# Two half-height products side by side in the score stage of differential attention

## The chip, the core and the metric

The kernel runs on one NeuronCore of a Trainium2 chip. The metric is the device time of one execution in microseconds (us); lower is better. The median of three runs of the kernel before is 1331.72 us (1330.39 to 1333.47).

## The reference

One decoder layer of 1024 tokens and width 1024: one input projection, a group of four differential-attention heads and a group of eight sparse-attention heads, an output projection, a layer norm, a SwiGLU feed-forward layer and a second layer norm. The change touches the differential heads alone. Each has two parts `c` with queries and keys of 64 dimensions; their two softmax maps share the values and are subtracted:

```python
def block(args):                     # 128 query rows
    qi, q_blk = args
    ...
    s = jnp.einsum('bqhcd,bkhcd->bhcqk', q_blk, k).astype(f32) * scale
    s = s - slopes[None, :, None, None, None] * dist
    p = masked_softmax(s, dist >= 0)
    a = p[:, :, 0] - lam * p[:, :, 1]
    return jnp.einsum('bhqk,bkhe->bqhe', a.astype(dt), v)
```

## The kernel before

**Two-term numbers.** Large products work on float32r operands. A float32 tensor is split into a high term and the low rest, and a product of two such tensors is made of three products, high by high, high by low and low by high (`mm3`, lines L118 to L120).

**Scores.** A score product has only 64 dimensions, so the 128 rows of the array hold both terms of the key at once. For part 0 of a head, `kd[0]` has the key's high term in partitions 0 to 63 and its low term in 64 to 127; for part 1, `kd[1]` has them the other way round (`evac_k`). A query tile `q` holds its high term twice, once in each half of the partitions, in columns 0 to 511, and its low term twice in columns 512 to 1023 (`evac_q` writes one copy, and `move`, L163, makes the others with DMAs). `q_of` returns the two column ranges of a block of 128 query rows as `q[0]` (high) and `q[1]` (low).

`scores` then needs two products per chunk. The first (L313) is the high query by both terms of the key; the second (L314) is the low query by both terms of the key, and accumulates onto the first in one score bank of PSUM:

```python
nc.tensor.matmul(ps[:, :c + part], lhsT=q[0], rhs=k[:, ks], start=True, stop=False)
nc.tensor.matmul(ps[:, :c + part], lhsT=q[1], rhs=k[:, ks], start=False, stop=True)
```

**Chunks and banks.** A unit is one head and one block `i` of 128 query rows. Its width is `(i + 1) * 128` keys. A width up to 512 is one chunk, a greater one is two of equal size, so chunks have 128, 256, 384, 512, and twice 320, 384, 448 or 512 columns. Over four heads there are 48 chunks per part, 96 in all. There are two score banks (`ps_s`, tag S). For each chunk VectorE reads the bank, adds the distance term, writes the scores to a tile `t` and keeps the running minimum (L320); its last minimum is the bias of the exponential on ScalarE (`exps`, L334). A bank is free for the next chunk when L320 has read it.

**Order.** `front` of a unit (in `diff_units`) makes the scores and exponentials of part 0, then of part 1, then combines them (L451 to L457, VectorE and GpSimd). `back` transposes the combined map (L343), multiplies by the values (L470) and collects the head's output. The back of a unit is written one or two units after its front. Between them lie fillers: projections of later heads and of the output layer, whose products (L118 to L120 into the banks psM) have a lower priority, and which a pump deals out at a rate for each phase. The framework's scheduler sets each engine's final order from priorities and a model of the timeline. Each engine runs its instructions in that order, TensorE's weight loads (PEld in the profile) being able to run ahead of its products.

Of the kernel before, what the change touches and what calls it, by code (L numbers as in the profile page):

```python
# [11 lines left out]
F32 = mybir.dt.float32  # L12
F32R = mybir.dt.float32r
AF = mybir.ActivationFunctionType
ALU = mybir.AluOpType
AX = mybir.AxisListType

P = 128
# [21 lines left out]
def layer_kernel(ctx: ExitStack, tc: tile.TileContext, xT, x, w_t, w_vg, w_dv, lam_in, subln,  # L40
# [4 lines left out]
    nc = tc.nc  # L45
# [7 lines left out]
    def ps_s():  # L53
        return psum.tile([P, 512], F32, tag="S", name="psS", bufs=2)

    def ps_t():
        return psum.tile([P, 512], F32, tag="T", name="psT", bufs=3)

    def ps_o():
        return psum.tile([P, 512], F32, tag="O", name="psO", bufs=1)  # L60
# [85 lines left out]
    with ExitStack() as ctx_a:  # L146
        pa = ctx_a.enter_context(tc.tile_pool(name="pa", bufs=1))

        def small(shape, tag, bufs, dt=F32):
            return pa.tile(shape, dt, tag=tag, name=tag, bufs=bufs)  # L150
# [101 lines left out]
        dsel = pa.tile([P, 1024], F32, tag="dsel", name="dsel", bufs=1)  # L252
# [44 lines left out]
        def q_of(qt, i, a):  # L297

            q = qt[1 + i // 4][a]
            c = (i % 4) * P  # L300
            return q[:, c:c + P], q[:, 512 + c:512 + c + P]

        def scores(q, k, k0, width, dist, slope, m, t, cmp=None):

            c = NC if cmp else 0
            n = (c + width + 511) // 512
            w = -(-(c + width) // (32 * n)) * 32
            part, at = width - (n - 1) * w, 0
            m0 = None
            for h in range(n):  # L310
                ps = ps_s()
                ks = slice(k0 + at, k0 + at + part + c)
                nc.tensor.matmul(ps[:, :c + part], lhsT=q[0], rhs=k[:, ks], start=True, stop=False)  # L313
                nc.tensor.matmul(ps[:, :c + part], lhsT=q[1], rhs=k[:, ks], start=False, stop=True)  # L314
                if c:
                    k0 += c
                    nc.vector.tensor_tensor_reduce(out=cmp[0], in0=ps[:, :c], in1=cmp[1], scale=slope, scalar=3.0e38,
                                                   op0=ALU.add, op1=ALU.min, accum_out=cmp[2])
                m1 = m if h == n - 1 else pa.tile([P, 1], F32, tag="m0", name="m0", bufs=4)
                nc.vector.tensor_tensor_reduce(out=t[:, at:at + part], in0=ps[:, c:c + part],  # L320
                                               in1=dist[:, at:at + part], scale=slope,
                                               scalar=3.0e38 if h == 0 else m0, op0=ALU.add, op1=ALU.min,
                                               accum_out=m1)
                at, part, c, m0 = at + part, w, 0, m1

        def t_tiles(width):

            if width <= 512:
                t = pa.tile([P, 1024], F32, tag="t", name="t", bufs=6)
                return [t[:, 0:512], t[:, 512:1024]]  # L330
            return [pa.tile([P, 1024], F32, tag="t", name="t", bufs=6) for _ in range(2)]

        def exps(t, width, m, r):
            nc.scalar.activation(t[:, :width], t[:, :width], AF.Exp, bias=m, scale=-1.0, accum_out=r)  # L334
# [4 lines left out]
        def transposed_whole(srcs):  # L339

            tp = ps_t()
            for n, s in enumerate(srcs):
                nc.tensor.transpose(tp[:, n * P:(n + 1) * P], s, ident)  # L343
            w = len(srcs) * P
            pt = pt_tile(F32)
            nc.scalar.copy(pt[:, :w], tp[:, :w])
            return pt
# [84 lines left out]
        def diff_units(h, qt, kd, V):  # L432
            slope = SLOPES[h]
            state = {}

            def make(i):
                hf, i4 = divmod(i, 4)
                width = (i + 1) * P
                ts = []

                def front():
                    m = small([P, 2], "m", 4)
                    if i4 == 0:
                        state["r0", hf] = small([P, 4], "r0", 2)
                    r0, r1 = state["r0", hf][:, i4:i4 + 1], small([P, 1], "r1", 4)
                    ts.extend(t_tiles(width))
                    for c in range(2):
                        scores(q_of(qt, i, c), kd[c], 0, width, dsel[:, 1024 - width:], slope, m[:, c:c + 1], ts[c])
                        exps(ts[c], width, m[:, c:c + 1], r1 if c else r0)

                    nc.vector.reciprocal(r1, r1)  # L451
                    nc.vector.scalar_tensor_tensor(r1, r0, lam[:, 0:1], r1, op0=ALU.mult, op1=ALU.mult)
                    cut = width * 5 // 8
                    nc.vector.scalar_tensor_tensor(ts[0][:, :cut], ts[1][:, :cut], r1, ts[0][:, :cut],
                                                   op0=ALU.mult, op1=ALU.add)
                    nc.gpsimd.tensor_scalar(ts[1][:, cut:width], ts[1][:, cut:width], r1, None, op0=ALU.mult)
                    nc.gpsimd.tensor_add(ts[0][:, cut:width], ts[0][:, cut:width], ts[1][:, cut:width])  # L457

                def back(fill):
                    if i4 == 0:  # L460
                        state["orow"] = small([P, 4, P], "od", 2)
                        state["ss"] = small([P, 4], "ss", 2)
                    orow, ss = state["orow"], state["ss"]
                    po = ps_o()
                    for j4 in range(0, i + 1, 4):
                        js = range(j4, min(j4 + 4, i + 1))
                        pt = transposed_whole([ts[0][:, j * P:(j + 1) * P] for j in js])
                        for n, j in enumerate(js):
                            c = (j % 4) * 256 + (h % 2) * P
                            nc.tensor.matmul(po[:, :P], lhsT=pt[:, n * P:(n + 1) * P], rhs=V[j // 4][:, c:c + P],  # L470
                                             start=(j == 0), stop=(j == i))
                        fill((j4 + len(js)) / (i + 1))
                    tmp = small([P, P], "ms", 2)
                    nc.vector.tensor_copy(orow[:, i4, :], po[:, :P])
                    nc.scalar.activation(tmp, po[:, :P], AF.Square, accum_out=ss[:, i4:i4 + 1])
                    if i4 == 3:
                        late.append(lambda: finish(orow, ss, state["r0", hf]))

                def finish(orow, ss, r0):

                    nc.vector.tensor_mul(r0, r0, r0)
                    nc.vector.tensor_scalar(r0, r0, EPS, None, op0=ALU.mult)
                    nc.vector.scalar_tensor_tensor(ss, ss, 1.0 / P, r0, op0=ALU.mult, op1=ALU.add)
                    nc.gpsimd.tensor_tensor(ss, ss, mhalf[:, :4], op=ALU.pow)
                    nc.vector.tensor_mul(orow, orow, ss.unsqueeze(2).to_broadcast([P, 4, P]))
                    tp = ps_t()
                    for n in range(4):
                        nc.tensor.transpose(tp[:, n * P:(n + 1) * P], orow[:, n, :], ident)
                    for n in range(2):
                        md = small([P, 256], "tmp", 3)  # L490
                        nc.scalar.activation(md, tp[:, n * 256:(n + 1) * 256], AF.Copy, scale=g08)
                        b = hf * 4 + n * 2
                        nc.sync.dma_start(mix_d[b:b + 2, :, h, :].rearrange("i p t -> p i t"),
                                          md.rearrange("p (i t) -> p i t", t=P))

                return front, back, 2.0 * (i + 1) + 1

            return [make(i) for i in range(NB)]
# [186 lines left out]
        for hf in range(2):  # L685
            ps3 = [f() for f in (ps_s, ps_m, ps_t)]
            for k in range(KT):
                ks = slice(k * P, (k + 1) * P)
# [7 lines left out]
        kd = [[] for _ in range(4)]  # L696
# [4 lines left out]
        for k0, nk in ((0, 3), (3, 3), (6, 2)):  # L701
            n = nk * 280
# [10 lines left out]
        for i in range(NB):  # L713
# [3 lines left out]
            ps = ps_t()  # L717
# [82 lines left out]
        for make, fillers, due, after, look in phases:  # L800
# [26 lines left out]
            at = 0.0  # L827
# [390 lines left out]
```

## Time and profile before

| | |
|---|---|
| median of 3 runs | 1331.72 us |
| the profiled execution | 1330.62 us |
| its span, first to last instruction | 1328.9 us |
| granted TensorE clock, mean | 0.997 |
| TensorE busy | 1301.0 us (98%) |
| VectorE / ScalarE / GpSimd busy | 914.5 / 649.7 / 467.4 us |
| score products of all heads, L313 and L314 | 304 and 304 |

Busy time is the union of an engine's instructions. A line of a group reads: source line, engine, operation, output and inputs, shapes and count, then busy time in us, mean duration in ns, idle time just before, and what ended that idle time. A line of a timeline begins with the start and the duration in us. TensorE's products overlap in the pipeline, so a product's duration is longer than the distance to the next start.

### The profile page before, as it was taken

The page shows a single profiled execution, that of the slowest core. Times are in us where ns is not written, and L with a number is a line of the kernel's source. Part 1 is how long each engine was busy: PE and PEld are TensorE (multiplying, and loading weights), DVE is VectorE, ACT ScalarE, POOL GpSimd, SP SyncE. Part 2 cuts the span into 40 slices and gives each one's busy share as a digit, 9 for nine tenths or more (in the row PEclk, how much of TensorE's full clock was granted, in tenths as well). Part 3 has the DMA queues.
Part 4 walks back from the last instruction along what each step waited for, and adds up shares of the span by engine and source line. Part 5 has one row for each costly group of instructions (what it writes and reads, how often), then busy time and mean ns, then how long its engine had stood idle before and what let it go on. Part 6 is the DMA issues. An engine that isn't in the chain of part 4 may idle for free.

```text
span 1328.9 us, 20439 instructions
## 1 busy us (share of the span) xinstructions
PE 1301.0 (98%) x6922; PEld 1106.2 (83%) x6922; DVE 914.5 (69%) x1949; ACT 649.7 (49%) x1398; POOL 467.4 (35%) x504
## 2 busy tenths in 40 slices
PE   9999999999999999999999999999999999999997
PEld 7898998888889878888877888888888888888886
DVE  5536658678798466684687768777767768555588
ACT  5336678676787456652335332332333326533430
POOL 4414354354445336553522232222312232000072
PEclk9999999999999999999999999999999999999999
DMA  9412022130211325532313666655455549868641
GB/s 360 132 27 63 7 59 50 31 80 19 61 25 45 72 59 156 174 113 103 103 64 101 210 203 223 204 168 190 158 192 188 188 152 340 278 200 285 194 171 64
DMA packets 86842, 183.13 MB, mean 138 GB/s; under 512 B 10577, under 2 KB 19153, under 8 KB 86609
## 3 DMA queue, kind: packets, MB, share of 16 engines
q1 hardware_dynamic: 86736, 181.82, 42.4%
q8 instruction: 55, 0.90, 0.3%
q14 instruction: 51, 0.41, 0.1%
HBM read 116.18 MB, written 57.15 MB: 130 GB/s over the span
## 4 chain that ended last, share of the span: by engine, by line
PE 90%; DVE 4%; ACT 2%; DMA 2%; issue 2%; SPq 0%; POOLq 0%; DVEq 0%; POOL 0%; ACTq 0%
PE psM L118 10%; PE psM L120 10%; PE psM L119 10%; PE psT L118 6%; PE psT L119 6%; PE psT L120 6%; PE psS L120 6%; PE psS L118 6%; PE psS L119 6%; PE psT L353 4%; PE psS L313 3%; PE psS L314 3%; PE psO L416 2%; PE psO L470 2%; PE psO L414 2%; PE psO L118 2%
## 5 line engine op out<-in xcount | busy, mean ns | idle before, releaser
L334 ACT ACTIVATE t<-t,m 128x128 f32<-128x128 f32 (+7 forms) x192 | 144.0, 751 | 69.7 <-DVE m L320 66.2
L399 POOL TENSOR_SCALAR t<-t,r,gates 128x640 f32<-128x640 f32 (+7 forms) x128 | 99.6, 784 | 189.3 <-DVE r L393 103.9
L118 PE MATMUL psM<-big,w 128*128 128x512 f32 x304 | 121.9, 401 | 0.5 <-ACT w L83 0.3
L313 PE MATMUL psS<-slot,q 128*128 128x320 f32 (+10 forms) x304 | 113.7, 376 | 8.0 <-DVE m L320 5.3
L119 PE MATMUL psM<-big,w 128*128 128x512 f32 x304 | 119.9, 394 | 0.7 <-POOL big L85 0.7
L120 PE MATMUL psM<-big,w 128*128 128x512 f32 x304 | 119.8, 395 | 0.0
L979 POOL TENSOR_TENSOR half<-half,half 128x512 f32<-128x512 f32 x22 | 33.1, 1502 | 197.6 <-ACT half L978 197.6
L85 DVE TENSOR_TENSOR pt<-psT,pt 128x512 fp32r<-128x512 f32 (+1 forms) x152 | 91.1, 612 | 13.4 <-ACT pt L83 12.8
L314 PE MATMUL psS<-slot,q 128*128 128x320 f32 (+10 forms) x304 | 99.4, 329 | 0.0
L83 ACT CAST pt<-psT 128x512 fp32r<-128x512 f32 (+1 forms) x152 | 77.1, 527 | 32.6 <-PE psT L353 24.0
L83 ACT CAST big<-slot 128x1024 fp32r<-128x1024 f32 (+1 forms) x54 | 54.1, 1018 | 67.5 <-DVE slot L971 58.7
L85 DVE TENSOR_TENSOR op<-op 128x1024 fp32r<-128x1024 f32 x44 | 60.9, 1393 | 35.7 <-ACT op L83 35.3
L353 PE MATMUL psT<-ident,t 128*128 128x128 f32 x528 | 84.0, 274 | 1.4 <-DVE pt L85 0.9
L85 DVE TENSOR_TENSOR big<-slot,big 128x1024 fp32r<-128x1024 f32 (+1 forms) x54 | 63.9, 1191 | 29.2 <-ACT big L83 29.0
L313 PEld LDWEIGHTS psS<-slot,q 128*128 128x128 f32 x304 | 57.4, 189 | 23.1 <-DVE m L320 13.7
L83 ACT CAST op<-op 128x1024 fp32r<-128x1024 f32 x44 | 46.0, 1052 | 60.8 <-DMA op<-t_d 58.4
L320 DVE CUSTOM_DVE_ANT_0 t<-psS,dsel 128x384 f32<-128x384 f32 (+9 forms) x128 | 62.4, 493 | 16.3 <-PE psS L314 15.4
L416 PE MATMUL psO<-pt,slot 128*128 128x256 f32 x264 | 72.9, 299 | 0.3
L983 POOL TENSOR_TENSOR half<-half,half 128x512 f32<-128x512 f32 x22 | 36.5, 1659 | 102.7 <-DVE half L982 102.5
L414 PE MATMUL psO<-pt,slot 128*128 128x256 f32 x264 | 71.0, 288 | 0.1
L118 PEld LDWEIGHTS psM<-big,w 128*128 128x128 f32 x304 | 57.3, 188 | 12.8 <-ACT w L83 1.0
L353 PEld LDWEIGHTS psT<-ident,t 128*128 128x128 f32 x528 | 61.7, 140 | 7.4 <-issue 3.2
(368 smaller groups left out, 3944.9 us busy)
## 6 DMA issues: line engine op xcount, KB each, us to landing
a_d<-slot SPq DMA_DIRECT2D x77, 256.0 KB, 3.0
t_d<-slot SPq DMA_DIRECT2D x77, 256.0 KB, 2.2
q<-q SPq DMA_DIRECT2D x48, 256.0 KB, 2.9
slot<-in_w_up_dram SPq DMA_DIRECT2D x22, 512.0 KB, 3.8
slot<-in_w_down_dram SPq DMA_DIRECT2D x22, 512.0 KB, 3.9
op<-a_d SPq DMA_DIRECT2D x44, 256.0 KB, 4.0
op<-t_d SPq DMA_DIRECT2D x44, 256.0 KB, 4.6
big<-a_d SPq DMA_DIRECT2D x33, 256.0 KB, 3.0
```

Of the source, the lines that this page charges most:

```text
L83: nc.scalar.copy(hi, src)
L85: eng.tensor_sub(lo, src, hi.bitcast(F32))
L118: nc.tensor.matmul(acc, lhsT=ah, rhs=bh, start=first, stop=False, skip_group_check=more)
L119: nc.tensor.matmul(acc, lhsT=ah, rhs=bl, start=False, stop=False, skip_group_check=more)
L120: nc.tensor.matmul(acc, lhsT=al, rhs=bh, start=False, stop=last, skip_group_check=more)
L313: nc.tensor.matmul(ps[:, :c + part], lhsT=q[0], rhs=k[:, ks], start=True, stop=False)
L314: nc.tensor.matmul(ps[:, :c + part], lhsT=q[1], rhs=k[:, ks], start=False, stop=True)
L334: nc.scalar.activation(t[:, :width], t[:, :width], AF.Exp, bias=m, scale=-1.0, accum_out=r)
L353: nc.tensor.transpose(tp[:rows, n * P:(n + 1) * P], s, ident)
L399: nc.gpsimd.tensor_scalar(t, t, r[:, c:c + 1], gates[:, i, gc:gc + 1], op0=ALU.mult, op1=ALU.mult)
L414: nc.tensor.matmul(po[:, :256], lhsT=v, rhs=pt[:, 0, n * 256:(n + 1) * 256], start=False, stop=False)
L416: nc.tensor.matmul(po[:, :256], lhsT=v, rhs=pt[:, 1, n * 256:(n + 1) * 256], start=False, stop=last)
```

## The change

The differential heads' fronts call a new function, `scores_both`, once for both parts instead of `scores` once for each. For a chunk it takes both score banks, one for each part, and makes the two first products as before. The second products are now of 64 rows: low query by high key alone. The high key of part 0 lies in partitions 0 to 63 and that of part 1 in 64 to 127, so that one uses the upper and the other the lower half of the array, each writing its own bank. The product of the two low terms is left out. `tc.issue_after(last.ins)` orders both behind the second of the first products on TensorE. Then VectorE empties both banks. The exponentials of both parts follow after all chunks.

```diff
+        def scores_both(qs, ks, width, slope, m, ts):
+            n = (width + 511) // 512
+            w = -(-width // (32 * n)) * 32
+            part, at = width - (n - 1) * w, 0
+            m0 = [None, None]
+            for h in range(n):
+                cs = slice(at, at + part)
+                ps = [ps_s()[:, :part] for _ in range(2)]
+                for c in range(2):
+                    last = nc.tensor.matmul(ps[c], lhsT=qs[c][0], rhs=ks[c][:, cs], start=True, stop=False)
+                with tc.issue_after(last.ins):
+                    for c in range(2):
+                        own = slice(c * 64, c * 64 + 64)
+                        nc.tensor.matmul(ps[c], lhsT=qs[c][1][own, :], rhs=ks[c][own, cs], start=False, stop=True)
+                for c in range(2):
+                    m1 = m[:, c:c + 1] if h == n - 1 else pa.tile([P, 1], F32, tag="m0", name="m0", bufs=4)
+                    nc.vector.tensor_tensor_reduce(out=ts[c][:, cs], in0=ps[c], in1=dsel[:, 1024 - width + at:][:, :part],
+                                                   scale=slope, scalar=3.0e38 if h == 0 else m0[c], op0=ALU.add,
+                                                   op1=ALU.min, accum_out=m1)
+                    m0[c] = m1
+                at, part = at + part, w
...
                     ts.extend(t_tiles(width))
+                    scores_both([q_of(qt, i, c) for c in range(2)], kd, width, slope, m, ts)
                     for c in range(2):
-                        scores(q_of(qt, i, c), kd[c], 0, width, dsel[:, 1024 - width:], slope, m[:, c:c + 1], ts[c])
                         exps(ts[c], width, m[:, c:c + 1], r1 if c else r0)
```

## The prediction

> **What bounds the kernel now.** I read the page first, then the stretches of the four differential heads, then single products.
>
> ```profile
> span 1328.9 us, 20439 instructions
> ...
> PE 1301.0 (98%) x6922; PEld 1106.2 (83%) x6922; DVE 914.5 (69%) x1949; ACT 649.7 (49%) x1398; POOL 467.4 (35%) x504
> ...
> PEclk9999999999999999999999999999999999999999
> ...
> PE 90%; DVE 4%; ACT 2%; DMA 2%; issue 2%; SPq 0%; POOLq 0%; DVEq 0%; POOL 0%; ACTq 0%
> ```
>
> TensorE is busy 98% of the span at full clock, and 90% of the chain that ended last is TensorE. So TensorE's time counts nearly one for one, where TensorE is what holds. The differential heads run from about 400 to 600 us. The next view is that of stretches (busy time by engine, instructions in brackets), and below it the second products (L314) alone in two of them:
>
> ```profile
> 413.00:488.00 75.00, 74.73 (x448) 65.83 (x447) 40.05 (x125) 36.96 (x101) 31.28 (x32) 1.00 0.25 61
> 488.00:527.00 39.00, 33.56 (x206) 28.34 (x205) 28.81 (x76) 25.19 (x66) 26.04 (x26) 0.99 0.45 131
> 527.00:544.00 17.00, 17.00 (x118) 16.36 (x117) 8.82 (x36) 9.13 (x32) 5.43 (x9) 0.91 0.48 132
> 544.00:575.00 31.00, 28.16 (x163) 22.40 (x161) 22.67 (x68) 21.98 (x53) 20.69 (x18) 1.00 0.61 196
> 575.00:600.00 25.00, 25.00 (x139) 21.61 (x138) 19.73 (x47) 12.61 (x29) 11.92 (x10) 1.00 0.27 86
> ...
> 488.00:527.00 39.00, 6.14 (x18) 3.43 (x18) 0.99 0.45 131
> ...
> 544.00:575.00 31.00, 7.25 (x21) 3.98 (x21) 1.00 0.61 196
> ```
>
> In three stretches TensorE has no idle time. In 488–527 it idles 5.4 us and in 544–575 2.8 us, 8.3 us in all; 39 of the 96 second products, some 20 of 48 pairs, lie there. Who holds it there, by the waits between 400 and 600 us (total, times, longest) and the chain:
>
> ```profile
> PEld psS L313 <- DVE m L320: 6.8, 13, 1.1
> ...
> PE psS L313 <- DVE m L320: 2.4, 5, 0.8
> ...
> 517.29 3.76 DMA q<-q
> ...
> 521.12 4.91 DMA q<-q
> ```
>
> 9.2 us are waits for VectorE to empty a score bank, and one late pair of q copies holds the chain from 517 to 526 us.
>
> **The change, part by part.** The second products keep their number, 96; each pair now has 64 rows per product and shares the array. Groups by shape, 400 to 600 us (busy us, mean ns), then single TensorE products (start, duration), and the weight loads beside the first of them:
>
> ```profile
> L314 PE MATMUL psS<-slot,q 128*128 128x512 f32 x24 | 9.5, 395 | 0.0
> ...
> L314 PE MATMUL psS<-slot,q 128*128 128x384 f32 x24 | 8.1, 337 | 0.0
> ...
> L314 PE MATMUL psS<-slot,q 128*128 128x448 f32 x16 | 5.8, 365 | 0.0
> ...
> L314 PE MATMUL psS<-slot,q 128*128 128x320 f32 x16 | 4.9, 308 | 0.0
> ...
> L314 PE MATMUL psS<-slot,q 128*128 128x256 f32 x8 | 2.2, 281 | 0.0
> ...
> L314 PE MATMUL psS<-slot,q 128*128 128x128 f32 x8 | 2.1, 279 | 0.0
> ```
>
> ```profile
> 451.10 0.28 PE L314 MATMUL psS<-slot,q 128*128 128x128 f32 x1
> 451.21 0.27 PE L313 MATMUL psS<-slot,q 128*128 128x128 f32 x1
> ...
> 464.84 0.41 PE L313 MATMUL psS<-slot,q 128*128 128x512 f32 x1
> 465.09 0.40 PE L314 MATMUL psS<-slot,q 128*128 128x512 f32 x1
> 465.32 0.39 PE L313 MATMUL psS<-slot,q 128*128 128x512 f32 x1
> 465.55 0.40 PE L314 MATMUL psS<-slot,q 128*128 128x512 f32 x1
> ...
> 488.62 0.36 PE L314 MATMUL psS<-slot,q 128*128 128x448 f32 x1
> 488.82 0.37 PE L313 MATMUL psS<-slot,q 128*128 128x448 f32 x1
> ...
> 551.72 0.34 PE L314 MATMUL psS<-slot,q 128*128 128x384 f32 x1
> 551.89 0.34 PE L313 MATMUL psS<-slot,q 128*128 128x384 f32 x1
> 552.08 0.34 PE L314 MATMUL psS<-slot,q 128*128 128x384 f32 x1
> ```
>
> ```profile
> 465.09 0.19 PEld L313 LDWEIGHTS psS<-slot,q 128*128 128x128 f32 x1
> 465.32 0.19 PEld L314 LDWEIGHTS psS<-slot,q 128*128 128x128 f32 x1
> ```
>
> What a product costs the stream is the distance between starts, not its duration: 0.11 us at 128 columns, 0.18 at 384 (0.17 and 0.19), 0.20 at 448, 0.23 at 512; I take 0.12 at 256 and 0.15 at 320 between them.
>
> *Removed, at best:* one of each pair's two streams. Pairs by width: 4, 4, 8, 12, 8, 12 (128, 256, 320, 384, 448, 512). 4×0.11 + 4×0.12 + 8×0.15 + 12×0.18 + 8×0.20 + 12×0.23 = 8.6 us. *At worst:* a load starts with the product before it (465.32), one ahead, and the narrowest products come no closer than 0.11 us though 128 columns should need a quarter of what 512 do. If the lower half's load follows the upper half's in the same way, the second product starts 0.11 us behind the first, and a pair saves its spacing less 0.11: 0, 0.01, 0.04, 0.07, 0.09, 0.12. That is 4×0.01 + 8×0.04 + 12×0.07 + 8×0.09 + 12×0.12 = 3.4 us. I take 3.4, since the 0.11 is a row.
>
> *Added: two changes of the array's shape per pair,* from 128 rows to two halves and back, 96 in all. No row has one. The nearest rows are products whose loads have 64 columns (form 128*64), among ones with 128:
>
> ```profile
> 95.67 0.27 PE L353 MATMUL psT<-ident,pc 128*64 128x128 f32 x1
> 95.78 0.27 PE L353 MATMUL psT<-ident,t 128*128 128x128 f32 x1
> 95.89 0.27 PE L353 MATMUL psT<-ident,pc 128*64 128x128 f32 x1
> ```
>
> They follow each other at 0.11 us: fewer columns cost nothing, the lower end (0 us). But their sums still run through all 128 rows. With two halves each column of the array gives two sums to two banks, where the product before gives one, so a reason stands for the array to be empty between them. A 512-column product ends 0.165 us after its successor starts (0.395 less 0.23); if the successor may not start until then, 96×0.165 = 15.8 us. If the next load may not run ahead either, 0.19 more each, 34.0 us: the upper end. A gain is excluded, since nothing is taken away at a change of shape. I take 15.8: rows, not columns, is what the sum passes through, which leaves the zero row the wrong kind, while the loads in this trace always run ahead.
>
> On such a change the Trainium skill, "TensorEngine Tiling (Array Packing)", Key Properties, says that a new tiling mode, as against another tile of the same mode, drains the engine. By that rule the sum is the one below; without it the first rival's; no run here shows a change of mode.
>
> *Moved: order.* Before, a part's two chunks went through the two score banks and its exponentials began; now a chunk takes both banks for both parts at once. Evictions, exponentials, loads and DMAs stay the same in number, and none moves past SP's or POOL's queue. The second main product waits for the second bank, and by the added order both halves wait behind it, with all that TensorE's queue holds after them. VectorE per eviction and ScalarE per exponential:
>
> ```profile
> L334 ACT ACTIVATE t<-t,m 128x1024 f32<-128x1024 f32 x8 | 9.2, 1155 | 8.6 <-DVE m L320 8.5
> ...
> L320 DVE CUSTOM_DVE_ANT_0 t<-psS,dsel,m 128x512 f32<-128x512 f32 x8 | 6.0, 749 | 1.1 <-PE psS L314 0.9
> ```
>
> Where projection products are at hand they fill the wait, at no cost. Where they have run out (the 20 pairs), VectorE finds no scores from its last eviction until a main product, the halves and their tail are through: 0.23 + 0.23 + 0.17 = 0.63 us a pair, 12.6 us at most. The first part's exponential starts one eviction (0.75 us) later, and the second's follows it by 1.16 us. The lower end is 0: the same banks are emptied as often, so the 9.2 us of waits don't vanish. I take 2 us, a quarter of the 8.3 us that TensorE idles there; if the cover in the other 28 pairs were gone too, 28×0.63 = 17.6 us more.
>
> **The sum.** −3.4 + 15.8 + 2 = 14.4 us. In the 20 pairs with idle time around them the net addition (0.33 − 0.07 us each, 5.2 us) is half hidden: −2.6. So +11.8 us on the profiled execution's own 1330.6 us (its span and 1.7 us around it): 1342. The median of the runs shown, 1331.72, is 1.1 us above that execution, well inside the range.
>
> **The rivals.** *No price on the change of shape (faster, the other side).* For it speak the rows at 95.67 us. The saving is 3.4 to 8.6 us, of which the 20 pairs keep half (×0.79): 2.7 to 6.8 less 2 us of waits, so −0.7 to −4.8, 1326 to 1330, middle 1328. It decides from the point where a change of shape costs under 3.4/96 to 8.6/96, that is 35 to 90 ns.
>
> *Emptying, and no load ahead.* Against it: every load here starts beside a running product (465.32). 34.0 − 3.4 + 2, less half of 20×0.64: +26, 1357. The Trainium skill, "TensorE: Matmul & The Clock Gate", Part 3 (what overlaps and what doesn't), lets a load overlap products in flight only in other row groups, which would give this rival. The trace differs for whole-array products: the load at 465.32 starts with the product of the same rows.
>
> *The halves don't run side by side.* Each takes its full stream and the shape is free: no gain, 2 to 5 us of waits, 1333 to 1336. Nothing in the trace speaks for or against.
>
> *A small price, 35 to 90 ns.* Gain and price cancel: 1329 to 1334.
>
> **How the numbers follow.** Emptying at both changes: 0.37. No price: 0.36, on both sides of the bound below. Emptying without loads ahead: 0.11. No side by side: 0.08. Small price: 0.08. I forecast 1342, the likeliest; with its dearer variant emptying has 0.48. This kernel's runs spread from 1330.39 to 1333.47, 0.23%, so under 0.2% (2.7 us) is no change. Faster: two thirds of the no-price case and a sliver of the small price, 0.26. Same: the rest of no price, most of small price, half of no side by side, 0.22. Slower: 0.52. The range 1326 to 1357 leaves out the upper half of the dearest case (0.06) and the best of no price (about 0.07), and some of each end for the 0.23% between runs; the forecast's own range is 1335 to 1350.
>
> **What would show it.** Distance from the second main product's start to the first half's: 0.40 us at 512 columns says emptying, 0.23 none, over 0.5 also a load held back. From the first half's start to the second's: near 0 says parallel loads, 0.11 one after the other, 0.23 no side by side. From the second half to the next whole product: 0.40 or 0.23 again. TensorE's waits for VectorE at the first main product (L313's now 9.2 us) and its idle in the two stretches (8.3 us) show the cost of the order. The forecast is wrong if starts keep their 0.23 us across the change of shape, or if TensorE's order in the stretches came out so differently that waits outweigh both.

## The result, and the profile after

The changed kernel takes 1345.57 us in the median (1341.72 to 1346.87) against 1330.62 us for the kernel before in the same comparison: a ratio of 1.0103, 95% interval 1.009 to 1.0117. It is slower by 14.95 us in the medians. The profiled execution of the changed kernel took 1344.78 us, 14.2 more than the one before.

The page of the kernel after, lines that answer to those of before:

```profile
span 1343.0 us, 20440 instructions
...
PE 1313.7 (98%) x6922; PEld 1101.4 (82%) x6922; DVE 904.2 (67%) x1949; ACT 650.7 (48%) x1398; POOL 464.2 (35%) x504
...
PE 86%; DVE 5%; DMA 3%; ACT 3%; issue 2%; POOL 1%; SPq 0%; POOLq 0%; DVEq 0%; ACTq 0%
```

TensorE has as many products as before and is busy 12.7 us longer; its idle time, the span less the busy time, grows by 1.4 us, from 27.9 to 29.3. VectorE, ScalarE and GpSimd have not grown by more than 1 us. So nearly all of the time is TensorE's, although the chain that ended last runs through TensorE for 86% and not 90%. The timeline of the kernel after (start, duration) shows one pair of 512 columns and one of 384. L337 is the first product, L341 the half-height one; x2 is two products in a row:

```profile
410.37 0.63 PE L337 MATMUL psS<-slot,q 128*128 128x512 f32 x2
410.93 0.49 PE L341 MATMUL psS<-slot,q 64*128 64x512 f32 x2
411.36 0.39 PE L440 MATMUL psO<-pt,slot 128*128 128x256 f32 x1
411.58 0.27 PE L438 MATMUL psO<-pt,slot 128*128 128x256 f32 x1
411.69 0.28 PE L440 MATMUL psO<-pt,slot 128*128 128x256 f32 x1
...
421.12 0.51 PE L337 MATMUL psS<-slot,q 128*128 128x384 f32 x2
421.56 0.44 PE L341 MATMUL psS<-slot,q 64*128 64x384 f32 x2
421.93 0.39 PE L118 MATMUL psM<-slot,big 128*128 128x256 f32 x1
422.15 0.28 PE L119 MATMUL psM<-slot,big 128*128 128x256 f32 x1
```

And the weight loads around the first pair, with a group of the half-height products (busy time, mean ns):

```profile
410.25 0.31 PEld L337 LDWEIGHTS psS<-slot,q 128*128 128x128 f32 x2
410.93 0.18 PEld L341 LDWEIGHTS psS<-slot,q 64*128 64x128 f32 x2 [0.36 <-issue]
411.35 0.19 PEld L440 LDWEIGHTS psO<-pt,slot 128*128 128x128 f32 x1 [0.24 <-DVE pt L85]
411.46 0.19 PEld L438 LDWEIGHTS psO<-pt,slot 128*128 128x128 f32 x1
...
L341 PE MATMUL psS<-slot,q 64*128 64x512 f32 x24 | 6.8, 520 | 0.0
```

The reader is to see four things.

1. The halves do run side by side, in 47 of the 48 pairs; in one (441.27 and 442.50) other products stand between them. Two halves are one row of 0.49 us, and 24 products of 520 ns are 6.8 us of busy time, little more than half of 24×0.52. In the trace the second starts 3 ns after the first, and both loads stand in one 0.18 us.
2. On entering, two first products and the way to the halves take 410.93 − 410.37 = 0.56 us. One spacing of 512 columns is 0.23, so the second first product holds the halves off for 0.33 us, 0.10 more than the 0.23 that a whole product would wait.
3. From the halves to the next product 0.43 us pass (411.36 − 410.93), 0.20 more than the halves' own stream.
4. That next product of 256 columns takes 0.22 us to its successor (411.58 − 411.36), where the one after it takes 0.11: 0.10 more. Its load begins with it at 411.35, not one product ahead as the load at 411.46 does. The row names VectorE for that load's wait, but the excess is the same before other next products (the table below).

Median distances between starts in this trace, in us, over those pairs whose distances hold no wait and no spell at a lower clock (some 30 of the 48):

| columns | pairs | whole product's spacing | to the halves | halves to the next | next one's excess | lost per pair |
|---|---|---|---|---|---|---|
| 128 | 4 | 0.11 | 0.205 | 0.255 | 0.10 | 0.23 |
| 256 | 4 | 0.12 | 0.21 | 0.31 | 0.10 | 0.26 |
| 320 | 8 | 0.147 | 0.242 | 0.339 | 0.10 | 0.24 |
| 384 | 12 | 0.174 | 0.268 | 0.369 | 0.10 | 0.21 |
| 448 | 8 | 0.20 | 0.297 | 0.397 | 0.10 | 0.19 |
| 512 | 12 | 0.227 | 0.327 | 0.425 | 0.10 | 0.17 |

"Lost" is the three columns after the spacing, less three spacings (of the four before, one stays in front of the pair). Taken for all 48 pairs, the sum is 4×0.23 + 4×0.26 + 8×0.24 + 12×0.21 + 8×0.19 + 12×0.17 = 10.0 us. Every visit to the half shape costs 0.34 us (128 columns) to 0.40 us (512) and saves one spacing, and no spacing is that long. That leaves 4 us or more of the 14 to 15, for waits that come of the new order or for the clock. The waits first: totals, times and longest between 400 and 645 us in the kernel after:

```profile
DVE t L344 <- PE psS L341: 40.9, 33, 4.9
...
PEld psS L341 <- issue: 11.0, 42, 0.4
...
PEld psS L337 <- DVE m L344: 8.9, 16, 1.2
...
PE psS L337 <- DVE m L344: 4.5, 7, 0.9
```

VectorE waits 40.9 us for scores (19.7 before). A wait of TensorE for a bank can stand in two rows, that of the load (PEld) and that of the product behind it (PE): in this trace every such gap of a product lies within one of its load. So the two rows are not to be added. TensorE's products waited 4.5 us for banks, where they waited 2.4 us before.

How waits and clock add up shows in a count over all starts. For each product, take the distance to the next start; what goes beyond the usual distance for its columns (0.109 us at 128, else the table's or the median of the trace before) is sorted by where it lies. In us:

| | before | after |
|---|---|---|
| usual distances of all products | 1263.1 | 1255.0 |
| beyond them, beside the half-height products | 0 | 26.3 |
| beyond them, in spells at half the clock | 1.6 | 5.0 |
| beyond them, elsewhere | 53.3 | 45.9 |
| first to last start | 1318.0 | 1332.2 |

By the table of distances, the visits are 18.6 of the 26.3 us (10.0 lost and 8.6 saved), which leaves 7.7 for waits beside them, and elsewhere waits are 7.4 us fewer. Waits on the whole are as long as before (+0.3). So the 14.2 us of the profiled execution are 10.5 from the shape (18.6 less the 8.1 of the first line) and 3.4 from the clock: three spells of 3.4 us at half speed where the kernel before has one. The last section has their rows.

### The profile page after: what moved, and what is told of

Its sections match the earlier page's. It is cut to its first block, busy times and chain, and to the rows that moved or that the text cites. A ratio compares the mean times of both kernels' runs of the same rounds, so it can differ in the third digit from the quotient of the medians.

```text
span 1343.0 us, 20440 instructions
## 1 busy us (share of the span) xinstructions
PE 1313.7 (98%) x6922; PEld 1101.4 (82%) x6922; DVE 904.2 (67%) x1949; ACT 650.7 (48%) x1398; POOL 464.2 (35%) x504
## 4 chain that ended last, share of the span: by engine, by line
PE 86%; DVE 5%; DMA 3%; ACT 3%; issue 2%; POOL 1%; SPq 0%; POOLq 0%; DVEq 0%; ACTq 0%
PE psM L118 10%; PE psM L120 10%; PE psM L119 10%; PE psT L118 6%; PE psT L119 6%; PE psT L120 6%; PE psS L120 5%; PE psS L119 5%; PE psS L118 5%; PE psT L377 4%; PE psS L313 2%; PE psO L440 2%; PE psO L438 2%; PE psO L494 2%; PE psO L120 2%; PE psO L118 2%
## 5 line engine op out<-in xcount | busy, mean ns | idle before, releaser
L313 PE MATMUL psS<-slot,q 128*128 128x320 f32 (+8 forms) x208 | 77.0, 372 | 3.3 <-DVE m L320 2.9
L83 ACT CAST op<-op 128x1024 fp32r<-128x1024 f32 x44 | 45.9, 1051 | 60.9 <-DMA op<-t_d 56.9
L118 PEld LDWEIGHTS psM<-big,w 128*128 128x128 f32 x304 | 57.6, 190 | 14.5 <-ACT w L83 1.2
L83 ACT CAST big<-big 128x1024 fp32r<-128x1024 f32 (+1 forms) x49 | 44.6, 915 | 47.0 <-DMA big<-t_d 37.8
L119 PEld LDWEIGHTS psM<-big,w 128*128 128x128 f32 x304 | 57.7, 190 | 11.8 <-issue 0.6
L120 PEld LDWEIGHTS psM<-big,w 128*128 128x128 f32 x304 | 57.4, 189 | 11.7 <-issue 1.0
```

What stands on the lines that cost most here:

```text
L83: nc.scalar.copy(hi, src)
L118: nc.tensor.matmul(acc, lhsT=ah, rhs=bh, start=first, stop=False, skip_group_check=more)
L119: nc.tensor.matmul(acc, lhsT=ah, rhs=bl, start=False, stop=False, skip_group_check=more)
L120: nc.tensor.matmul(acc, lhsT=al, rhs=bh, start=False, stop=last, skip_group_check=more)
```

## The experiments

Two theories stood after this. *Price of the shape:* each change costs TensorE 0.10 us of emptying and 0.10 us of a weight load that could not run ahead, whatever lies inside a visit. *Order:* taking both banks before either is emptied costs the rest. A third, the clock, stands as a rival in the first expectation. The rivals are in the expectations.

**Order alone, whole products.** This kernel keeps the changed order and banks, with second products of 128 rows:

```diff
-                        nc.tensor.matmul(ps[c], lhsT=qs[c][1][own, :], rhs=ks[c][own, cs], start=False, stop=True)
+                        nc.tensor.matmul(ps[c], lhsT=qs[c][1], rhs=ks[c][:, cs], start=False, stop=True)
```

> The order and the banks of the change, with second products of all 128 rows as before: no change of the array's shape. Theory (price of the shape): the changed kernel's trace accounts for some 10.2 us of its 15 us by distances between starts around the half-height products, so the order alone should cost the rest, 4 to 5 us: 1335 us. Rival (the order does most of it, the distances only shift waits): 1340 to 1345 us. Rival (the order is free, the rest being the clock's short half-speed spells): 1331 us.

Measured: 1335.42 us against 1331.61, ratio 1.0040 (1.0024 to 1.0055). With whole products the order costs about 4 us, as expected; it is not free. Its waits, 400 to 600 us:

```profile
PEld psS L337 <- DVE m L343: 9.4, 17, 1.2
...
PE psS L337 <- DVE m L343: 4.7, 8, 1.0
PEld psS L337 <- DMA q<-q: 3.5, 1, 3.5
PE psS L337 <- DMA q<-q: 3.3, 1, 3.3
```

Again a load's row and a product's row show the same waits; the 3.5 and 3.3 us for the copies of `q` are one. TensorE's products waited 4.7 us for banks (2.4 before) and 3.3 us for `q` copies (2.1 before). TensorE's idle time over the whole span grew from 27.9 to 31.9 us, which is all that the order costs here, and the trace has one half-speed spell, like the one before. So these waits belong to the order, not to the half shape. In the changed kernel they don't stand on top: its waits on the whole have hardly grown. That longer products fill waits is seen in the next experiment.

**Half-height products, each alone.** The order of before; only the rows of the second product are cut (`own` is the half that holds the part's high key):

```diff
-                nc.tensor.matmul(ps[:, :c + part], lhsT=q[1], rhs=k[:, ks], start=False, stop=True)
+                nc.tensor.matmul(ps[:, :c + part], lhsT=q[1][own, :], rhs=k[own, ks], start=False, stop=True)
```

> The order before the change, each second product of 64 rows but alone between two whole products: 96 visits to the half shape instead of 48, nothing saved. Theory: 0.10 us more on entering, 0.30 us more on leaving, whatever is inside: 96 x 0.40 = 38 us, 1369 us, or 1362 where idle time hides a part. Rival (what costs is two products together, in two banks or two loads, not the shape): 1331 us, distances of 0.23 us at 512 columns. Rival (only the return to whole products costs): 1350 to 1360 us.

Measured: 1354.39 us, ratio 1.0184 (1.016 to 1.0207), 22.8 us more. Its timeline:

```profile
466.58 0.42 PE L313 MATMUL psS<-slot,q 128*128 128x384 f32 x1
466.92 0.44 PE L314 MATMUL psS<-slot,q 64*128 64x384 f32 x1
467.29 0.44 PE L313 MATMUL psS<-slot,q 128*128 128x384 f32 x1
467.66 0.43 PE L314 MATMUL psS<-slot,q 64*128 64x384 f32 x1
468.03 0.71 PE L470 MATMUL psO<-slot,pt 128*128 128x128 f32 x4
```

Distances of 0.34 to 0.37 us stand where 0.18 stood before, so a single half pays the full price and pairing is not what costs. The total alone would also fit the rival that only the return to whole products costs. But where no other half stands just before, a half of 384 columns still starts 0.27 us behind the whole product and not 0.17 (six cases), so entering costs too. The total missed the expectation of 1362 to 1369. The reason shows in the stretch of 400 to 631 us, first here, then in the kernel before:

```profile
400.00:631.00 231.00, 230.07 (x1197) 176.70 (x1198) 133.47 (x398) 120.72 (x314) 102.34 (x108) 0.98 0.34 94
```

```profile
400.00:631.00 231.00, 222.13 (x1333) 193.06 (x1333) 146.69 (x412) 125.45 (x327) 113.69 (x114) 0.99 0.36 104
```

Before, TensorE idled 8.9 us in it; here 0.9. The longer products filled its waits, and more than these 8 us, since short waits are covered by the recorded durations. By the count over all starts, 38.7 us stand beside the half products, as expected; elsewhere the excess falls from 53.3 to 35.2 us, by 18.1; and the half-speed spells (10.2 us here, 3.4 before) take 4.2 us more. Together that is 24.8 us, and the profiled execution is 24.7 us longer than the one before.

**Each pair twice in one visit.** The low term is counted twice:

```diff
-                    for c in range(2):
+                    for c2 in range(4):
+                        c = c2 % 2
...
+                        nc.tensor.matmul(..., start=False, stop=c2 > 1)
```

> The changed kernel with each pair of half-height products issued twice in a row, so that the low term is counted twice: 96 pairs in the same 48 visits. Theory (a price per visit): the second pair costs its stream alone, 8.6 us in all: 1354 us, second pair 0.23 us behind the first at 512 columns. With loads not running ahead inside the half shape, 0.11 us more per pair, 1359 us. Rival (a price per half-height product): 0.40 us more per second pair, 19 us on top: 1373 us.

Measured: 1352.33 us, ratio 1.0161 (1.0146 to 1.0176), 0.58% or 7.7 us above the changed kernel's ratio, where a price per visit gives 8.6 and a price per product 28. Its timeline, to be set against the one at 410.93 above:

```profile
410.25 0.73 PE L342 MATMUL psS<-slot,q 64*128 64x512 f32 x4
410.91 0.39 PE L441 MATMUL psO<-pt,slot 128*128 128x256 f32 x1
411.13 0.28 PE L439 MATMUL psO<-pt,slot 128*128 128x256 f32 x1
```

Two pairs take 0.66 us where one took 0.43: 0.23, exactly one stream. The starts inside the x4 row say where the rest lies (medians at 512 columns): the second pair starts 0.337 us behind the first, 0.11 more than a stream and not the 0.23 that was expected, and the next whole product 0.327 us behind the second pair, 0.10 more. So of the 0.20 us on leaving, half falls to the first pair alone, whose load was not hidden, and half to the change back. The second pair has the same rows as the first, and its load was hidden. In these traces loads run ahead inside a shape and are held at a change of it.

**Half of the load.** The halves load 64 columns of the low query instead of 128, so half the score rows lack the low term:

```diff
-                    last = nc.tensor.matmul(..., start=True, stop=False)
+                    last = nc.tensor.matmul(..., start=True, stop=True)
...
-                        nc.tensor.matmul(ps[c], lhsT=qs[c][1][own, :], rhs=ks[c][own, cs], ...)
+                        nc.tensor.matmul(ps[c][0:64], lhsT=qs[c][1][own, 0:64], rhs=ks[c][own, cs], ...)
```

> The changed kernel with half-height products that load 64 of the 128 columns of the low query, so that half of the rows of scores lack the low term: the load takes half the time, all else stays. Theory (the load of the halves stands open in the visit): some 0.05 us less per visit, 48 x 0.05 = 2.6 us, 1343 us, and the distance from the halves to the next whole product falls from 0.42 to 0.37 us at 512 columns. Rival (emptying alone, the load runs ahead): 0.42 us and 1345 us.

Measured: 1341.97 us, ratio 1.0078 (1.006 to 1.0096), 0.25% or 3.3 us below the changed kernel's ratio. The two intervals overlap, and the granted clock differed too (0.9965 in the median of the runs, 0.9935 for the changed kernel). The timeline decides:

```profile
410.61 0.45 PE L341 MATMUL psS<-slot,q 64*64 64x512 f32 x2
410.99 0.38 PE L441 MATMUL psO<-pt,slot 128*128 128x256 f32 x1
411.21 0.28 PE L439 MATMUL psO<-pt,slot 128*128 128x256 f32 x1
```

0.38 us to the next product, not 0.43 (medians at 512 columns 0.375 and 0.425): 0.05 us are gone with half of the load, whose own row falls from 0.18 to 0.13 us. A shorter tail of the products is not the reason by the rows before: products whose loads have 64 columns last 0.27 us there, like those of 128 (95.67). This agrees with the doubled pairs: of the 0.20 us on leaving, 0.10 is the halves' own open load. The other 0.10, and the 0.10 on entering, I call emptying: a wait of fixed length that no load accounts for. The next whole product's open load is the 0.10 behind it.

**Parts alternating, no bank held.** Whole products again and both exponentials last, but each bank gets both of its products before the other's begin:

```diff
                 for c in range(2):
+                    ps = ps_s()[:, :part]
+                    nc.tensor.matmul(ps, lhsT=qs[c][0], rhs=ks[c][:, cs], start=True, stop=False)
+                    nc.tensor.matmul(ps, lhsT=qs[c][1], rhs=ks[c][:, cs], start=False, stop=True)
                     m1 = ...
```

> Whole second products, parts alternating chunk by chunk and both exponentials last as in the change, but each bank gets both of its products before the other part's begin: no bank is held half done and no order is added. The order with both banks held measured 1335.4 us against 1331.6. Theory (the joint hold of both banks is what the order costs): 1331 to 1332 us. Rival (the alternation and the later exponentials cost it): 1335 us, like the order with both banks held.

Measured: 1324.81 us against 1330.78, ratio 0.9955 (0.9943 to 0.9967): faster than the kernel before, which neither theory had. So the order's 4 us are two things: alternating with both exponentials last gains 6 us, and holding both banks by the added order costs 10 to 11 (medians and ratios). A little of the gain may be the clock's: against the five runs before that were granted 0.997 or 0.998, as all of these were, it is 5.4 us.

```profile
PEld psS L337 <- DVE m L340: 4.6, 11, 0.7
PE psS L337 <- DVE m L340: 1.8, 6, 0.4
...
488.00:527.00 39.00, 37.64 (x242) 32.45 (x241) 28.83 (x86) 27.15 (x74) 26.81 (x29) 1.00 0.48 139
```

TensorE's products wait 1.8 us for banks (2.4 before, 4.7 with both held) and next to nothing for `q` copies (2.1 before). In 488–527 TensorE idles 1.4 us where it idled 5.4, though not the same work lies there (242 products, 206 before).

**Both banks taken, no order added.** As the first experiment, without `tc.issue_after`:

```diff
-                with tc.issue_after(last.ins):
-                    for c in range(2):
+                for c in range(2):
```

> Whole second products, both banks taken for a chunk before either is emptied, but without the added order that puts both second products behind the second first product. With the added order 1335.4 us, without the joint hold 1324.8. Theory (it is the joint hold of the banks that costs 10 us): 1333 to 1336 us. Rival (the added order costs it, by keeping the first bank's second product waiting for the second bank): 1325 to 1328 us.

Measured: 1327.06 us, ratio 0.9973 (0.9963 to 0.9983), so the theory as I wrote it fell. In this kernel's order 41 of 48 pairs have each second product right behind its own first; only 7 still do both first products before. Left free, the scheduler undoes the joint hold: the added order is what makes it, and with it go 8 to 9 us. The two can't be told apart by these runs. Why this kernel stays 2 to 3 us behind the alternating one is not shown.

**Alternating, part 0's exponential early.** The alternating kernel, with this inside its chunk loop instead of the exponentials behind it:

```diff
+                    if h == n - 1:
+                        exps(ts[c], width, m[:, c:c + 1], rs[c])
```

> The alternating order that measured 1324.8 us, with part 0's exponential written right behind its last chunk instead of behind both. Theory (the gain over before, 6 us, is from alternating the parts, with waits on q copies and banks gone): 1323 to 1326 us. Rival (the gain is from the later exponentials): back to 1331 us.

Measured: 1328.52 us, ratio 0.9988 (0.998 to 0.9997). It lies between the two, nearer to the rival. Most of the gain goes with the late exponentials: with them 0.9955, without 0.9988. Why a later exponential helps stays open; the traces only show that without it the products' waits for banks grow again, to 3.0 us from 1.8.

**The alternating order again.** The same kernel, beside further runs of the kernel before:

> The alternating order again, unchanged, beside the kernel before on the same chip. Theory (the gain is the program's, not the chip's): ratio 0.994 to 0.997, 1325 us. Rival (the first measurement was a lucky set): ratio 0.998 to 1.001.

Measured: 1324.08 us, ratio 0.9953 (0.9941 to 0.9965). The gain is real, and this version beats both kernels.

**Only the widest chunks.** The change for units of 512 and 1024 keys alone:

```diff
+                    both = width in (512, 1024)
+                    if both:
+                        scores_both(...)
...
+                        if not both:
+                            scores(...)
```

> The change only for units of 512 and 1024 keys, whose chunks have 512 columns, the other units as before: 12 pairs that each save the most, a stream of 0.23 us. Theory (0.40 us per visit): 12 x 0.17 = 2.0 us lost, and a third of the order's 4 us, 1334 us. Rival (the widest chunks pay): 12 x 0.12 to 0.23 us gained, 1329 us.

Measured: 1335.59 us, ratio 1.0033 (1.0021 to 1.0045), 4.8 us more, against 3.4 expected. With the order that comes with it, even the widest chunk doesn't pay.

## Why the prediction was right, point by point

The forecast was 1342 us, +11.8 on the profiled execution; measured were +14.2 in the profile and +14.95 in the medians. The case it named, emptying at both changes of shape, is the one that happened, and its dearer variant is partly in it. Of the signs it named for 512 columns, the halves' starts came out near 0 apart as said; entering took 0.33 us where it said 0.40; leaving took 0.42 to 0.43 as said, but half of what is beyond a stream there is a held load. That the total came so close is in part luck: several terms were off, and their errors offset. Its terms:

- *Stream removed: taken as 3.4, measured as one full spacing per pair, 8.6 us.* The step "if the lower half's load follows the upper half's in the same way" failed: both loads ran together and the halves started 3 ns apart. The 0.11 us row is of loads into all 128 rows, and these go to different halves.
- *Change of shape: taken as 0.165 us each, 15.8 us; measured as up to 0.40 us per visit, 0.20 each, 18.6 us in all (10.0 lost and 8.6 saved).* Emptying is 0.10, not 0.165: the recorded overhang of a product is longer than what its successor must wait for. But "the loads in this trace always run ahead" failed at the change itself, for 0.10 us each. The two errors nearly cancel. The Trainium skill, "TensorEngine Tiling (Array Packing)", Key Properties, says that a changed tiling mode drains the engine; the trace agrees, with 0.10 us of emptying each way.
- *No load ahead: priced at 0.19 us each, measured 0.10.* The row's 0.19 us of a load includes a part that costs the stream nothing; 64 columns fewer took 0.05 us off. The Trainium skill, "TensorE: Matmul & The Clock Gate", Part 3, ties a load's overlap to other row groups. The doubled pair differs: its second load, of the same rows, was hidden. Here the condition is the shape, not the rows.
- *Order: taken as 2 us, measured about 4 net with whole products,* which is a gain of 5 to 6 and a loss of 10 to 11. The loss had been bounded at 12.6 us and the gain excluded by an argument ("the waits don't vanish"). The argument failed: with parts alternating and the exponentials last the products' waits for banks fell from 2.4 to 1.8 us, and that for `q` copies from 2.1 us to next to nothing. The 9.2 us in it were a misreading: they add the waits of loads and of products, which are the same waits.
- *Half of the addition hidden in idle stretches, −2.6:* this was of the right kind. The half-height products alone filled 18 us of waits, and in the changed kernel waits on the whole grew by 0.3 us and not by the 4 that the order costs alone.
- *The clock: not in the sum.* The changed kernel's trace has two more spells at half speed, worth 3.4 us.

By these sizes the sum for the profiled execution is −8.1 (the streams saved, as counted over all starts) + 18.6 + 0.3 + 3.4 = 14.2 us.

## What to carry to other kernels

Half-height products side by side save a stream only if enough of them follow each other without a whole product between: here a visit cost up to 0.40 us, so it must save more than that in streams, which by these numbers two pairs of 512 columns only just would (0.46; not run). Before pairing two accumulation groups, ask what the pairing makes wait: with two banks and whole products, filling both before either is emptied cost more than the order around it gained. Measure the order without the new operation: that led to the version that is faster. And when two costs are each measured alone, check by the trace whether they add up: here the order's 4 us and the shape's 10 make 14, the time that was to be explained, yet in the changed kernel's trace the waits hardly grew, and the rest is the clock.

## What the runs showed of the hardware that was not expected

Two loads into the upper and the lower half take the time of one (0.18 us). At the array's change of shape the next load is held back without any semaphore that the profile shows: the 0.36 us of the load queue's idle time at 410.93 have no releaser but "issue"; it is one of 42 such waits of the halves' loads, 11.0 us in all.

The clock shows short spells at half speed in this stage, and their number differs between kernels. Stretches of the kernel after, then of before:

```profile
500.00:505.00 5.00, 4.47 (x19) 3.31 (x20) 3.01 (x9) 2.16 (x6) 2.56 (x2) 0.66 0.20 52
...
510.00:515.00 5.00, 4.76 (x15) 3.54 (x15) 4.91 (x15) 3.15 (x14) 2.39 (x3) 0.66 0.13 38
```

```profile
525.00:530.00 5.00, 3.92 (x20) 3.92 (x21) 1.23 (x7) 2.34 (x8) 0.73 (x2) 0.66 0.57 131
```

A mean of 0.66 over 5 us is 3.4 us at half speed. The kernel before has one such spell, in the heads after a wait of 2 us for `q` copies; the one after has two in the heads and a third, of the same length, from 699 us on (a mean of 0.90 from 695 to 700 us and of 0.76 from 700 to 705). Each can cost up to 1.7 us, and the two more cost 3.4 us by the count over all starts.

The runs go the same way. Two runs of the changed kernel, granted 0.998 and 0.995 of the clock, took 1341.9 and 1341.7 us; one with 0.994 took 1344.8, and three with 0.993 took 1346.4 to 1346.9. The kernel before was granted 0.995 to 0.998 in its runs beside the experiments, and took 1327.6 to 1333.3. So at a clock that both kernels show the change costs 10 to 12 us, by two runs only, and some 3 to 5 us of the 14.95 in the medians are the clock's. What starts the spells was not tried, so whether the change brings them on stays open.
